# One transformer layer in split fp32: the first feed-forward chunk as seven block products, and modulation sums of 1024 columns

## The chip, the cores and the metric

The kernel runs on one NeuronCore of one Trainium2 chip. The metric is the device time of one execution in microseconds; of several executions the median counts. TensorE (PE) does matrix products, with its weight loads beside them (PEld); VectorE (DVE), ScalarE (ACT) and GpSimd (POOL) do elementwise work; SyncE (SP) and POOL issue most DMAs. Each engine runs its own instructions in order and waits for others at semaphores, so the order of the rows on each engine is part of the kernel.

## The reference, cut to what matters

One layer of a diffusion backbone is computed for 640 tokens: 128 context tokens and 512 latent ones, which share the weights but have modulations of their own (`c_ctx` and `c`). D_MODEL is 1024, D_FF 4096.

```python
def _modulation(cvec, w_mod, b_mod):
    m = jax.nn.silu(cvec) @ w_mod + b_mod
    return jnp.split(m[:, None, :], N_MOD, axis=-1)
...
    sh1, sc1, g1, sh2, sc2, g2 = _modulation(c, w_mod, b_mod)
    h = _rmsnorm(x, n1) * (1 + sc1) + sh1
...
    x = x + g1 * _merge(a_o, b_o, ga, gb, w_br_a, w_br_b, w_out)
    h2 = _rmsnorm(x, n2) * (1 + sc2) + sh2
    return x + g2 * _mlp(h2, w1, w2)
```

`_mlp` is a squared ReLU between two products: `relu(h2 @ w1)**2 @ w2`. A last RMSNorm follows. Everything is fp32.

## The kernel before, in words

**Data.** Activations lie feature-major: a tile holds 128 features of all 640 tokens, so a 1024-wide activation is eight tiles, f = 0 to 7. Tokens fall into two halves of 320, h0 and h1; h0 holds the 128 context tokens and 192 latent ones, and since their modulations differ, a modulated operation on h0 is a pair of 128 and 192 columns (`SEGS`). PE gets its precision by a split: each operand is a rounded high part and a low part (the rest), and a product of a 128x128 weight with 128x320 is three matmuls: high x high, high x low, low x high. ACT makes a weight's high part (L267, L1395), DVE or POOL its low part by a subtraction (L276, L273, L1400).

**Stages.** The input projection and two attentions fill the time to about 400 us. A merge follows: for each feature n two branch units per half, gated and added on DVE, whose sum is split into mh (ACT) and ml (DVE). From 449 us the output projection runs in units: `unit` (L1199) is 24 matmuls, eight k with three each, into one PSUM bank, called pss, pt or pg in rotation. Its order is features 0 to 3 with both halves, then h0 of 4 to 7, then h1 of 4 to 7. Behind each unit DVE adds the gated result to the residual x (`add_gated`, L1224), ACT squares it (L201), DVE sums the squares (L203). When a half is complete, two matmuls with ones (L208, L209), a logarithm and an exponential on ACT (L210, L211) make rstd, and the norm and modulation follow in steps on DVE and ACT: x times rstd and scale (xm, L336), high part with the shift added (hh0h to hh7h, L341), low part (hh0l to hh7l, L344).

**Late modulation.** The second half of the modulation map isn't done by PE. For each of 32 column tiles DVE multiplies rows of w_mod with a broadcast silu(cond) and sums along the row (L1102), in two halves of 512 columns for each of two conditions; `mods_done` adds the halves. `mod_pace` hands these sums out between the units by a running account of DVE time, MCOST a step; what is left is done when a step needs it.

**Feed-forward.** D_FF is worked off in four chunks of 1024. Layer 1 of chunk 0 was 16 plain units (eight output tiles, two halves), their weights through the class `Weights` (W), their ReLU and square into `hid_raw(0, ...)` (blocks 11, 12, 21, 22 by output parity and half). Everything after that runs as block products of Strassen's kind in Winograd's form, in the order of the list `SEQ`: a layer of a chunk is seen as 2x2 blocks (weight blocks by parity and k half, activation blocks by k half and token half) and done in seven products A11, A12, S3, A22, S2, S1, S4 instead of eight, each for n = 0 to 3. A product is 12 matmuls (four k with three each) into a bank of the eight-bank pool pp8. Its weights come through the class `Operands` (`OPS[0]`): A tiles are plain, B tiles are sums of two weight blocks, loaded by SP and added to by a DMA that POOL issues. Its activations are blocks and sums of blocks (B11, B21, T1 to T4, N22). For layer 1 these operands come from the split normed features: `t_pieces` adds hh-high and hh-low again, forms the differences and splits them anew, in small steps in the list `side`, of which one is taken after each product. POOL makes the low parts of A12 and A22 in layer 1.

**Order.** Up to `manual.close()` DVE's order is the order of the code; in the kernel before that call comes within or behind the plain feed-forward units. The other engines' order, and DVE's afterwards, is set by a list scheduler at build time.

Of the kernel before, what the change touches and what calls it, by code (L numbers as in the profile page):

```python
# [10 lines left out]
F32 = mybir.dt.float32  # L11
# [17 lines left out]
WP1 = 0  # L29
# [9 lines left out]
MCOST = 1500  # L39
LAG = (0, 4)  # L40
# [33 lines left out]
def trunk_layer(ctx: ExitStack, tc: tile.TileContext, xT, small_in, wmodA, wmodB, tabs, cacheK, cacheV, bias,  # L74
# [43 lines left out]

    def tt_tile(name):
        return cur["p"].tile([P, NT], F32R, tag="tt", bufs=12, name=name)  # L120
# [85 lines left out]
    def rstd_half(acc, last, rstd, sl):  # L206
        p, n = ps_t(), sl.stop - sl.start
# [3 lines left out]
        ACT.activation(rstd[:, sl], rstd[:, sl], AF.Exp, scale=-0.5)  # L211


    def w_order():
# [10 lines left out]
        for n in range(KT):  # L225
            yield ("w1", n), w1[n]
# [79 lines left out]
    WPOOLSET = {("out", n) for n in range(WPO, KT)} | {("w1", n) for n in range(WP1)}  # L306
    EXTRA = {("out", 4), ("w1", 0)}
# [781 lines left out]
    def late_mods():  # L1089

        cb = [tt_tile("cb") for _ in range(4)]
        for i in range(2):
            for q in range(2):
                MISC.dma_start(r32(cb[2 * q + i][:, :512]),
                               silu[i, 4 * q:4 * q + 4].rearrange("k p -> (k p)").partition_broadcast(P))
        for n in MODS:
            st = dp.tile([P, 1024], F32, tag="ms", bufs=3, name="wmt")
            DQ[QM].dma_start(st, wmodB[n])
            for q in range(2):
                for i in range(2):  # L1100
                    t = dp.tile([P, 512], F32, tag="mt", bufs=2, name="mt")
                    DVE.scalar_tensor_tensor(t, st[:, q * 512:(q + 1) * 512], 1.0, r32(cb[2 * q + i][:, :512]), op0=OP.mult,  # L1102
                                             op1=OP.mult, accum_out=parts[:, q, n, i:i + 1])
                if q == 0:
                    yield
# [121 lines left out]
    def norm_pieces(acc, last, rstd, h, apply):  # L1227
        return [lambda: None] * LAG[h] + [lambda: rstd_half(acc, last, rstd, HALVES[h])] + [lambda f=f: apply(range(f, min(f + NG, KT)))
                                                     for f in range(0, KT, NG)]

    def norm2(fs, h):
        mod_step(16 + 4 * (fs.stop + -fs.stop % MG) - lm_n[0])
        modulate([(H2[f], X1[f], mod(2, f), mod(1, f)) for f in fs], rstd2, h)

    X1 = {}
    acc2, rstd2 = u("acc2"), u("rstd2")
    H2 = [h_pair(f"hh{f}") for f in range(KT)]
    Wt = {}
    for n, h in order(KT, 4):
        if n not in Wt:  # L1240
            Wt[n] = W.get("out", n)
            X1[n] = o_tile(f"x1_{n}")
            nc.sync.dma_start(X1[n], xT[:, n, :])
        ps = unit(Wt[n], M, h)
        if h:
            W.done("out", n)
        add_gated(n, ps, h, 0)
        sq = sq_add(acc2, X1[n], n, HALVES[h])
        if n < KT - 4 or h == 0 and n < KT - 1:
            mod_pace(OU)  # L1250
        elif n == KT - 1:
            side += norm_pieces(acc2, sq, rstd2, h, lambda fs, h=h: norm2(fs, h))

    def final(fs, sl):
        for f in fs:
            DVE.tensor_mul(X1[f][:, sl], X1[f][:, sl], rstd3[:, sl])
            (nc.sync, nc.scalar)[f % 2].dma_start(yT[:, f, sl], X1[f][:, sl])

    def relu2(dst, src, h):

        r, sl = u("rl"), HALVES[h]
        ACT.activation(r[:, :HT], src, AF.Relu)
        if RL:
            ACT.activation(r[:, :HT], r[:, :HT], AF.Square)
            ACT.activation(dst[0][:, sl], r[:, :HT], AF.Copy)
        else:
            ACT.activation(dst[0][:, sl], r[:, :HT], AF.Square)

        def rest():
            if not RL:
                DVE.tensor_mul(r[:, :HT], r[:, :HT], r[:, :HT])
            DVE.tensor_sub(dst[1][:, sl], r[:, :HT], r32(dst[0][:, sl]))
        flush_later(posts)
        posts.append(rest)


    T = [{}, {}, {}]
    L0, L1 = slice(0, HT), slice(HT, NT)  # L1280

    def t_pieces(k):
        raw = {}

        def cut(dst, src, sl0, sl1):
            ACT.activation(dst[0][:, sl0], src, AF.Copy)
            later.append(lambda: DVE.tensor_sub(dst[1][:, sl1], src, r32(dst[0][:, sl0])))

        def p0():
            if k == 2:  # L1290
                mod_step(64 - lm_n[0])
            for i in range(3):
                T[i][k] = tt_tile(f"t{i + 1}_{k}")
            for i in range(2):
                raw[i] = u("hr")
                DVE.tensor_add(raw[i], r32(H2[k + 4 * i][0]), r32(H2[k + 4 * i][1]))
            raw[2] = u("t12")
            DVE.tensor_sub(raw[2][:, L0], raw[0][:, L1], raw[0][:, L0])
            cut((T[0][k], T[0][k]), raw[2][:, L0], L0, L1)
# [491 lines left out]
```

## Time and profile before

| | |
|---|---|
| runs shown | 928.15, 922.33, 924.48 us; median 924.48 |
| profiled execution | 927.14 us, of which the span of instructions 925.4 us |
| granted PE clock, mean | 0.996 |
| busy | PE 98%, PEld 95%, DVE 77%, ACT 61%, POOL 21% |
| DMA | 150.04 MB, mean 162 GB/s |

A row of the timeline gives the start in microseconds from the start of the span, the duration, the engine, the line of the kernel, the operation, result and operands by the program's names, and the shapes; a bracket at the end is the idle time ahead of it and what ended it. Matmuls overlap in the pipe, and so do, a little, instructions of DVE and ACT: the cost of one in a row of them is the distance of the starts. PEclk is the clock that PE was granted. A row of the windows gives, for a stretch of time, each engine's busy time and number of instructions.

### The profile page before, as it was taken

Reading aid. Unit: us, or ns where it says so; the run is one execution under the profiler, and the core shown is the slowest. Engines: PE = TensorE matmul, PEld = TensorE weight load, DVE = VectorE, ACT = ScalarE, POOL = GpSimd, SP = SyncE. Lnnn points to the kernel's source line nnn. Section 1 sums busy time; section 2 is a strip of 40 time slices with the busy share of each in tenths; the row PEclk is TensorE's granted clock in tenths of the full one; section 3 lists DMA queues with packets and bytes.
Section 4 is the critical chain, followed back from the end, with each engine's and each line's share of the span. In section 5 each row is a group of like instructions: output and inputs, shape, how many; then the busy total and the mean of one; then the engine's idle time right before and its main releaser. Section 6 shows DMA issues by size and latency. Waiting matters only on the chain.

```text
span 925.4 us, 16638 instructions
## 1 busy us (share of the span) xinstructions
PE 907.2 (98%) x6136; PEld 874.9 (95%) x6136; DVE 713.1 (77%) x1505; ACT 563.7 (61%) x1174; POOL 194.7 (21%) x224
## 2 busy tenths in 40 slices
PE   9999999999999999999999999999999999999996
PEld 7799889989999999999999999999999999999995
DVE  6675877857766697586789996985798769975897
ACT  4566767757656775665324667536764576447775
POOL 0020200002211011111130010354134532354140
PEclk9999999999999999999999999999999999999999
DMA  9883410115636389788843463898678876897575
GB/s 345 304 238 103 93 42 26 57 56 154 166 103 154 115 261 286 185 236 250 273 138 91 124 172 102 130 205 182 158 141 188 182 164 157 175 175 177 100 123 151
DMA packets 54177, 150.04 MB, mean 162 GB/s; under 512 B 6672, under 2 KB 10400, under 8 KB 54096
## 3 DMA queue, kind: packets, MB, share of 16 engines
q1 hardware_dynamic: 31440, 99.74, 32.5%
q0 software_dynamic: 21504, 47.93, 29.7%
q10 hardware_dynamic: 1152, 1.31, 0.4%
q8 instruction: 48, 0.79, 0.4%
q14 instruction: 33, 0.27, 0.1%
HBM read 136.62 MB, written 4.60 MB: 153 GB/s over the span
## 4 chain that ended last, share of the span: by engine, by line
PE 74%; DMA 8%; DVE 7%; ACT 5%; issue 4%; POOL 1%; SPq 0%; DVEq 0%; POOLq 0%; ACTq 0%
PE b L1659 10%; PE b L1660 10%; PE b L1658 10%; PE pg L315 6%; PE pg L316 6%; PE pg L317 6%; DMA wsb<-w 3%; PE pss L317 3%; PE pss L316 3%; PE pss L315 3%; PE pt L317 2%; PE pt L316 2%; PE pt L315 2%; DVE mt L1102 2%; PE pt L694 1%
## 5 line engine op out<-in xcount | busy, mean ns | idle before, releaser
L1395 ACT ACTIVATE wb<-wsb 128x512 fp32r<-128x512 f32 x140 | 87.0, 628 | 93.8 <-PE b L1660 57.7
L1659 PE MATMUL b<-op,wb 128*128 128x320 f32 x448 | 138.7, 310 | 1.3 <-DVE op L1468 1.3
L1658 PE MATMUL b<-op,wb 128*128 128x320 f32 x448 | 138.6, 309 | 0.6 <-ACT op L1467 0.6
L1660 PE MATMUL b<-op,wb 128*128 128x320 f32 x448 | 138.4, 309 | 0.0
L1400 DVE TENSOR_TENSOR wb<-wsb,wb 128x512 fp32r<-128x512 f32 x124 | 91.4, 740 | 32.3 <-ACT wb L1395 32.1
L1403 POOL DMA_DIRECT2D wsb<-w x84 | 73.7, 908 | 128.0 <-DVE wb L1400 99.8
L1659 PEld LDWEIGHTS b<-op,wb 128*128 128x128 f32 x448 | 84.1, 188 | 2.1 <-DVE op L1468 2.1
L1102 DVE SCALAR_TENSOR_TENSOR mt<-wmt,cb 128x512 f32<-128x512 f32 x128 | 80.7, 687 | 6.3 <-DMA wmt<-wmodB 6.2
L1658 PEld LDWEIGHTS b<-op,wb 128*128 128x128 f32 x448 | 84.2, 188 | 1.2 <-ACT op L1467 0.9
L1660 PEld LDWEIGHTS b<-op,wb 128*128 128x128 f32 x448 | 84.1, 188 | 0.0
L267 ACT ACTIVATE wh<-wst 128x512 fp32r<-128x512 f32 (+1 forms) x84 | 61.0, 740 | 32.9 <-PE pg L316 12.9
L276 DVE TENSOR_TENSOR wl<-wst,wh 128x512 fp32r<-128x512 f32 (+1 forms) x57 | 44.4, 789 | 15.0 <-ACT wh L267 13.0
L1380 POOL DMA_DIRECT2D wsb<-w x28 | 26.4, 944 | 139.0 <-DMA wsb<-w 51.7
L633 DVE TENSOR_TENSOR pl<-pt,ph 128x512 fp32r<-128x512 f32 (+1 forms) x72 | 44.9, 627 | 13.6 <-ACT ph L632 13.1
L632 ACT ACTIVATE ph<-pt 128x512 fp32r<-128x512 f32 (+1 forms) x72 | 39.2, 548 | 15.5 <-PE po L702 5.4
L1511 DVE SCALAR_TENSOR_TENSOR x<-b,parts,x 128x128 f32<-128x128 f32 (+1 forms) x116 | 46.3, 429 | 2.5 <-PE b L1660 1.6
L1658 PE MATMUL b<-t,wb 128*128 128x320 f32 x144 | 44.8, 311 | 0.4 <-DVE tp L1497 0.4
L1659 PE MATMUL b<-t,wb 128*128 128x320 f32 x144 | 44.5, 309 | 0.0
L1660 PE MATMUL b<-t,wb 128*128 128x320 f32 x144 | 44.5, 309 | 0.0
L1395 ACT ACTIVATE wb<-wst 128x512 fp32r<-128x512 f32 x56 | 34.7, 625 | 15.8 <-PE b L1660 8.8
L1468 DVE TENSOR_TENSOR op<-hid,op 128x1280 fp32r<-128x1280 f32 (+2 forms) x32 | 37.0, 1155 | 7.8 <-ACT op L1467 7.7
L1511 DVE SCALAR_TENSOR_TENSOR x<-tp,parts,x 128x320 f32<-128x320 f32 (+2 forms) x60 | 39.0, 679 | 1.0 <-ACT tp L1562 1.0
(886 smaller groups left out, 3010.2 us busy)
## 6 DMA issues: line engine op xcount, KB each, us to landing
wsb<-w POOLq DMA_DIRECT2D x112, 256.0 KB, 5.2
wst<-w SPq DMA_DIRECT2D x36, 512.0 KB, 3.9
wmt<-wmodB SPq DMA_DIRECT2D x32, 512.0 KB, 5.0
wst<-w_in SPq DMA_DIRECT2D x31, 512.0 KB, 4.2
wsb<-w SPq DMA_DIRECT2D x28, 512.0 KB, 4.3
ms<-wmodA SPq DMA_DIRECT2D x16, 512.0 KB, 7.7
wl<-w_in POOLq DMA_DIRECT2D x8, 512.0 KB, 7.8
wst<-w_br SPq DMA_DIRECT2D x8, 512.0 KB, 5.0
```

Source lines behind the costliest of these rows:

```text
L267: ACT.activation(hi[:, ks], st[:, ks], AF.Copy)
L315: PE.matmul(ps, wh[:, k], xh[:, sl], start=first, stop=False)
L316: PE.matmul(ps, wh[:, k], xl[:, sl], start=False, stop=False)
L317: PE.matmul(ps, wl[:, k], xh[:, sl], start=False, stop=last)
L1102: DVE.scalar_tensor_tensor(t, st[:, q * 512:(q + 1) * 512], 1.0, r32(cb[2 * q + i][:, :512]), op0=OP.mult, op1=OP.mult, accum_out=parts[:, ...
L1395: ACT.activation(w[:, 0:4], t, AF.Copy)
L1400: (nc.gpsimd if o in BLKPOOL[l - 1] else DVE).tensor_sub(w[:, 4:8], t, r32(w[:, 0:4]))
L1403: nc.gpsimd.dma_start(t, self.src(l, c, n, e)[:, 4 * half:4 * half + 4], accum_op=OP.add)
L1511: DVE.scalar_tensor_tensor(X1[i][:, sl], src[:, sl.start - off:sl.stop - off], g[:, j:j + 1], X1[i][:, sl], op0=OP.mult, op1=OP.add)
L1658: PE.matmul(b, w[:, k], xh, start=not whole and k == 0, stop=False, skip_group_check=True)
L1659: PE.matmul(b, w[:, k], xl, start=False, stop=False, skip_group_check=True)
L1660: PE.matmul(b, w[:, 4 + k], xh, start=False, stop=o not in ("A11", "S2", "S1") and k == 3, skip_group_check=True)
```

## The change

1. Layer 1 of chunk 0 goes through the seven block products too. The weights w1 of chunk 0 leave `Weights`; `FIRST0` begins with 28 products, among them three A11 products of layer 2 between S3 and S2. The four S3 products form a group: k 0 and 1 of all four, then k 2 and 3 of all four. In layer 2 of chunk 0, A12 gets a bank of its own and is added to the kept A11 by DVE (four more additions).
2. The operands come from unrounded normed features. `norm_first` (h0, four steps of two features) and `norm_last` (h1, four steps of two) scale on DVE and shift on ACT into raw tiles; `cut` splits a raw tile into parts on ACT and DVE; `t3_piece`, `t2_piece`, `t4_piece`, `t1_piece`, `n22_piece` form the differences from the raw tiles.
3. The modulation sums take 1024 columns each, 64 instead of 128 of 512; MCOST goes from 1500 to 1300 a step; all that are left are done with unit (6,0) of the output projection, where before the last of them ran beside the feed-forward units.
4. The PSUM pool of the units is closed, and pp8 opened, right behind the output projection; `manual.close()` moves there too. The pool of B tiles opens at unit (5,1).

```diff
         for n in range(KT):
             yield ("out", n), w_out[n]
-        for n in range(KT):
-            yield ("w1", n), w1[n]
...
     def mods_done(n0, n1):
         m = mods[:, n0:n1]
-        DVE.tensor_add(m, parts[:, 0, n0:n1], parts[:, 1, n0:n1])
...
-            for q in range(2):
-                for i in range(2):
-                    t = dp.tile([P, 512], F32, tag="mt", bufs=2, name="mt")
-                    DVE.scalar_tensor_tensor(t, st[:, q * 512:(q + 1) * 512], 1.0, r32(cb[2 * q + i][:, :512]), op0=OP.mult,
-                                             op1=OP.mult, accum_out=parts[:, q, n, i:i + 1])
-                if q == 0:
+            for i in range(2):
+                t = dp.tile([P, 1024], F32, tag="mt", bufs=1, name="mt")
+                DVE.scalar_tensor_tensor(t, st, 1.0, cb[i], op0=OP.mult, op1=OP.mult, accum_out=mods[:, n, i:i + 1])
+                if i == 0:
                     yield
...
+    def scaled(t, f, h):
+
+        off = HALVES[h].start
+        for sl, g in SEGS[h]:
+            d = t[:, sl.start - off:sl.stop - off]
+            DVE.scalar_tensor_tensor(d, X1[f][:, sl], mod(2, f)[:, g:g + 1], rstd2[:, sl], op0=OP.mult, op1=OP.mult)
+
+    def shifted(t, f, h):
+        off = HALVES[h].start
+        for sl, g in SEGS[h]:
+            d = t[:, sl.start - off:sl.stop - off]
+            ACT.activation(d, d, AF.Identity, bias=mod(1, f)[:, g:g + 1])
+
+    def norm_first(f0):
+
+        mod_step(16 + 4 * (f0 + 2) - lm_n[0])
...
+        for f, t in todo:
+            shifted(t, f, 0)
+            cut(H2[f][0][:, L0], H2[f][1][:, L0], t)
...
+    def cut(hi, lo, src):
+        ACT.activation(hi, src, AF.Copy)
+        later.append(lambda: DVE.tensor_sub(lo, src, r32(hi)))
...
+    def t3_piece(k):
+        r = t_new(2, k)
+        DVE.tensor_sub(r, RAW1[0][:, k + 4], RAW1[0][:, k])
+        cut_t(2, k, r)
...
-    FIRST0 = [("A11", 0), ("A11", 1), ("A11", 2), ("A12", 0), ("A12", 1), ("A11", 3), ("A12", 2), ("A12", 3)]
+    FIRST0 = [("A11", 0, 1), ("A11", 1, 1), ("A11", 2, 1), ("A12", 0, 1), ("A12", 1, 1), ("A11", 3, 1), ("A12", 2, 1),
+              ("A12", 3, 1), ("S3", 0, 1), ("S3", 1, 1), ("S3", 2, 1), ("S3", 3, 1), ("A11", 0), ("A11", 1), ("A11", 2),
+              ("S2", 0, 1), ("S2", 1, 1), ("S2", 2, 1), ("A22", 0, 1), ("S2", 3, 1), ("A22", 1, 1), ("A22", 2, 1),
+              ("A22", 3, 1), ("S1", 0, 1), ("S1", 1, 1), ("S4", 0, 1), ("S1", 2, 1), ("S4", 1, 1), ("S1", 3, 1),
+              ("S4", 2, 1), ("S4", 3, 1), ("A12", 0), ("A11", 3), ("A12", 1), ("A12", 2), ("A12", 3)]
...
             mod_pace(OU)
-        elif n == KT - 1:
-            side += norm_pieces(acc2, sq, rstd2, h, lambda fs, h=h: norm2(fs, h))
+        elif n == KT - 1 and h == 0:
+            side += [rstd2_half(sq, 0)] + [lambda f=f: norm_first(f) for f in range(0, KT, 2)]
+        if (n, h) == (5, 1):
             mod_step(64 - lm_n[0])
             pairs_pool()
...
     manual.close()
     banks.close()
     pp8.append(ctx.enter_context(tc.tile_pool(name="pp8", bufs=1, space=bass.MemoryType.PSUM, reuse_waits="tile")))
...
+    side += [lambda: None] * LAG2 + [rstd2_half(sq, 1)]
+    side += steps((norm_last, 0)) + steps((norm_last, 1), (t3_piece, 0)) + steps((norm_last, 2), (t3_piece, 1))
+    side += steps((norm_last, 3), (t3_piece, 2)) + steps((t3_piece, 3))
+    for f in (t2_piece, t4_piece, t1_piece, n22_piece):
+        for k in range(4):
+            side += steps((f, k))
```

Three places show how the rows move.

**PE, where the output projection ends.** pt is the bank of its last unit, (7,1); before, the next rows are plain feed-forward units, which read hh tiles and a weight w. With the waits of each row, before:

```order
L317 MATMUL pt<-mh,wl 128x320
L315 MATMUL pss<-hh0h,w_6148 128x320 [waits PE_49,Activation_49]
L316 MATMUL pss<-hh0l,w_6148 128x320 [waits DVE_49]
L317 MATMUL pss<-hh0h,w_6149 128x320 [waits DVE_49]
L315 MATMUL pss<-hh1h,w_6148 128x320 [waits Activation_49]
L316 MATMUL pss<-hh1l,w_6148 128x320
L317 MATMUL pss<-hh1h,w_6149 128x320
L315 MATMUL pss<-hh2h,w_6148 128x320 [waits Activation_49]
L316 MATMUL pss<-hh2l,w_6148 128x320 [waits DVE_49]
```

In the changed kernel b is a bank of pp8 and wb a block product's weight:

```order
L323 MATMUL pt<-mh,wl 128x320
L1646 MATMUL b<-hh0h,wb 128x320 [waits DVE_49,Activation_49]
L1647 MATMUL b<-hh0l,wb 128x320
L1648 MATMUL b<-hh0h,wb 128x320
L1646 MATMUL b<-hh1h,wb 128x320
L1647 MATMUL b<-hh1l,wb 128x320
L1648 MATMUL b<-hh1h,wb 128x320
L1646 MATMUL b<-hh2h,wb 128x320 [waits Activation_49]
L1647 MATMUL b<-hh2l,wb 128x320
L1648 MATMUL b<-hh2h,wb 128x320
L1646 MATMUL b<-hh3h,wb 128x320 [waits Activation_49]
L1647 MATMUL b<-hh3l,wb 128x320
```

Before, the first matmul waits for PE and ACT, and each low part's reader for DVE by itself. Now the first matmul waits for DVE, and the readers of hh0l to hh3l carry no wait for DVE any more.

**DVE, up to the gated add of unit (6,1).** x_6 is the residual of feature 6, xm a scaled feature, wl a plain weight's low part; before:

```order
L344 SCALAR_TENSOR_TENSOR hh5l<-xm,parts,hh5h 128x128
L344 SCALAR_TENSOR_TENSOR hh5l<-xm,parts,hh5h 128x192
L276 TENSOR_TENSOR wl<-wst,wh 128x1024
L1224 SCALAR_TENSOR_TENSOR x_5_6001<-pg,parts,x_5_6001 128x320
L1102 SCALAR_TENSOR_TENSOR mt,parts<-wmt,cb 128x512
L203 TENSOR_TENSOR acc_5642<-acc_5642,sq 128x320
...
L344 SCALAR_TENSOR_TENSOR hh7l<-xm,parts,hh7h 128x128
L344 SCALAR_TENSOR_TENSOR hh7l<-xm,parts,hh7h 128x192
L276 TENSOR_TENSOR wl<-wst,wh 128x1024
L1224 SCALAR_TENSOR_TENSOR x_6_6033<-pss,parts,x_6_6033 128x320
```

In the changed kernel, where raw is an unrounded feature and wb a block product's low part:

```order
L1391 TENSOR_TENSOR wb<-wst,wb 128x512 x2
L1225 SCALAR_TENSOR_TENSOR x_5_5902<-pg,parts,x_5_5902 128x320
L211 TENSOR_TENSOR acc_5560<-acc_5560,sq 128x320
L1601 TENSOR_SCALAR parts<-parts 128x16
L1274 TENSOR_TENSOR hh2l<-raw,hh2h 128x320
L1274 TENSOR_TENSOR hh3l<-raw,hh3h 128x320
L1274 TENSOR_TENSOR hh4l<-raw,hh4h 128x320
L1274 TENSOR_TENSOR hh5l<-raw,hh5h 128x320
...
L1240 SCALAR_TENSOR_TENSOR raw<-x_7_5973,parts,rstd_5561 128x192
L1391 TENSOR_TENSOR wb<-wst,wb 128x512
L1225 SCALAR_TENSOR_TENSOR x_6_5938<-pss,parts,x_6_5938 128x320
```

The gated add of (6,1) stands behind the low parts of hh2 to hh5, the scaling of features 6 and 7 and three low parts of block products; the modulation sums between are gone.

**DVE, ahead of the output projection.** sg and ml are the merge of feature 7; wl is a low part of an output weight. Before:

```order
L276 TENSOR_TENSOR wl<-wst,wh 128x1024
L1102 SCALAR_TENSOR_TENSOR mt,parts<-wmt,cb 128x512 x6
L1181 TENSOR_TENSOR sg<-pg,sg 128x320
L1181 TENSOR_TENSOR sg<-pss,sg 128x320
L1182 TENSOR_TENSOR sg<-sg 128x320
L1184 TENSOR_TENSOR ml<-sg,mh 128x320
```

In the changed kernel:

```order
L282 TENSOR_TENSOR wl<-wst,wh 128x1024
L1104 SCALAR_TENSOR_TENSOR mt,parts<-wmt,cb 128x1024 x4
L1182 TENSOR_TENSOR sg<-pg,sg 128x320
L1182 TENSOR_TENSOR sg<-pss,sg 128x320
L1183 TENSOR_TENSOR sg<-sg 128x320
L1185 TENSOR_TENSOR ml<-sg,mh 128x320
```

Six sums of 512 columns ahead of the merge of feature 7 became four of 1024.

More of the change, by code (lines that the diff above doesn't have):

```diff
@@ L38 @@
 NG = 2
[L39 to L40 removed]
+MCOST = 1300
+LAG2 = 2
 MAN = (0,)
@@ L1256, in final @@
[L1256 to L1276, printed above, removed]
@@ L1686, in trunk_layer @@
             side.pop(0)()
+    OPS[0].ahead()
+    todo = list(SEQ)
+    while todo:
+        group = [todo.pop(0)]
+        while todo and group[0][:2] == todo[0][:2] == (1, 0) and group[0][3] == todo[0][3] == "S3":
+            group.append(todo.pop(0))
+        jobs = []
+        for x in group:
+            l, c, n, o = x
+            w = OPS[0].get(x)
+            if l == 1:
+                xk = XN[o]
+            else:
+                t = opd(c, XOF[o])
+                xk = lambda k, t=t: (t[:, k], t[:, 4 + k])
+            p = pairs.setdefault((l, c, n), Pair())
+            whole = {"A12": "A11", "S1": "S2", "S4": "S2"}.get(o)
+            if (l, c, o) == (2, 0, "A12"):
+                whole = None
+            b = getattr(p, "b" + whole) if whole else bank()
+            setattr(p, "b" + o, b)
+            jobs.append((b, w, xk, o, whole, (l, c, n, o, b, p)))
+        if len(jobs) > 1:
+            flush_later()
+            for b, w, xk, o, whole, _ in jobs:
+                product(b, w, xk, o, whole, range(2))
+        for b, w, xk, o, whole, e in jobs:
+            product(b, w, xk, o, whole, range(2 if len(jobs) > 1 else 0, 4))
+            evict(*e)
     while side:
```

199 lines of the change are left out of this document (87 added, 112 removed).

## The prediction

> **What bounds the kernel now.** I read the page first: its span, the busy time by engine, the forty slices.
>
> ```profile
> span 925.4 us, 16638 instructions
> PE   907.2 (98%) x6136; PEld 874.9 (95%) x6136; DVE 713.1 (77%) x1505; ACT 563.7 (61%) x1174; POOL 194.7 (21%) x224
> PE   9999999999999999999999999999999999999996
> DVE  6675877857766697586789996985798769975897
> PEclk9999999999999999999999999999999999999999
> ```
>
> PE is busy in every slice at a full granted clock; no other engine is near that in the mean, though DVE comes close in slices 22 to 24, 486 to 555 us. Next I took the windows around the change: the output projection, the first feed-forward chunk, the products behind it (columns: stretch, length, busy time and instructions of PE, PEld, DVE, ACT, POOL, then clock, DMA share and GB/s).
>
> ```profile
> 449.00:507.00 58.00, 58.00 (x394) 57.68 (x393) 47.87 (x123) 20.80 (x39) 9.64 (x4) 1.00 0.50 165
> 507.00:563.00 56.00, 55.88 (x376) 54.98 (x375) 49.31 (x100) 34.36 (x73) 3.46 (x4) 1.00 0.45 123
> 563.00:617.00 54.00, 54.00 (x370) 54.00 (x369) 49.28 (x90) 31.15 (x56) 18.95 (x21) 1.00 0.77 162
> ```
>
> PE idles 0.12 us in these 168. So there is no stall for the change to recover: a gain can come only from matmuls that are no longer issued, and every wait that it adds shows in full. DVE is at 88% in the stretch that is rewritten, so its order decides whether PE stays fed.
>
> **What is removed.** Sixteen units of 24 matmuls become 28 products of 12: 384 - 336 = 48 fewer, and the rows of PE's order bear that out (5323 matmuls of 128x320 before, 5275 after). The group row offers a price, the timeline another:
>
> ```profile
> L1659 PE MATMUL b<-op,wb 128*128 128x320 f32 x448 | 138.7, 310 | 1.3 <-DVE op L1468 1.3
> 480.92 0.31 PE L315 MATMUL pss<-mh,wh 128*128 128x320 f32 x1
> 484.44 0.31 PE L315 MATMUL pg<-mh,wh 128*128 128x320 f32 x1
> 506.64 0.31 PE L315 MATMUL pss<-hh0h,w 128*128 128x320 f32 x1
> ```
>
> The mean of 310 ns is the time in which one matmul is in the pipe; two overlap. From 480.92 to 484.44 PE starts a whole unit of 24, so one costs 3.52/24 = 0.1467 us. The removed work is worth 48 x 0.1467 = **7.0 us**, not 48 x 0.31 = 14.9. That is 0.8% of 924, and about 1% is what a measurement of this kernel can tell from no change. The third row is the hand-over: the first feed-forward matmul starts at 506.64, right behind the last unit of the output projection.
>
> **What DVE's work does to the hand-over.** In the kernel before DVE is far behind there, and PE doesn't care:
>
> ```profile
> 513.09 0.54 DVE L1224 SCALAR_TENSOR_TENSOR x<-pss,parts,x 128x320 f32<-128x320 f32 x1
> 515.78 0.55 DVE L1224 SCALAR_TENSOR_TENSOR x<-pt,parts,x 128x320 f32<-128x320 f32 x1
> ```
>
> These are the gated adds of units (6,1) and (7,1), the last two of the output projection: 6.5 and 9.1 us after PE had passed on. The feed-forward units took banks of the same PSUM pool that were free, and the first four read only the first token half. In the changed kernel the pool is closed behind the output projection and the eight-bank pool opened, so the first product, A11(0), gets a bank that (6,1) still fills, and the third, A11(2), that of (7,1). The order shows it: A11(0)'s first matmul carries a wait on DVE, and the rows behind it, which read hh1l to hh3l, carry none, since the wait already reaches past these rows on DVE, to the gated add that is listed behind hh5l. So the time of that gated add is the first term, and I price DVE's and ACT's rows up to it by start-to-start times.
>
> ```profile
> 495.08 0.47 ACT L211 ACTIVATE rstd<-rstd 128x320 f32<-128x320 f32 x1
> 502.16 1.27 DVE L336 SCALAR_TENSOR_TENSOR xm<-x,parts,rstd 128x128 f32<-128x128 f32 x4
> 503.34 0.68 DVE L344 SCALAR_TENSOR_TENSOR hh2l<-xm,parts,hh2h 128x128 fp32r<-128x128 f32 x2
> 522.07 0.55 DVE L344 SCALAR_TENSOR_TENSOR hh2l<-xm,parts,hh2h 128x320 fp32r<-128x320 f32 x1
> 522.54 0.55 DVE L336 SCALAR_TENSOR_TENSOR xm<-x,parts,rstd 128x320 f32<-128x320 f32 x1
> 448.17 0.48 DVE L1181 TENSOR_TENSOR sg<-pg,sg 128x320 f32<-128x320 f32 x1
> 448.57 0.48 DVE L1181 TENSOR_TENSOR sg<-pss,sg 128x320 f32<-128x320 f32 x1
> 597.11 0.69 DVE L1400 TENSOR_TENSOR wb<-wsb,wb 128x512 fp32r<-128x512 f32 x1
> 597.71 0.67 DVE L1511 SCALAR_TENSOR_TENSOR x<-b,parts,x 128x128 f32<-128x128 f32 x2
> ```
>
> A pair of 128 and 192 columns costs 1.18/2 = 0.59, a scalar-tensor-tensor of 320 0.46, a tensor-tensor of 320 0.40, a weight's low part 0.60. The first half's rstd is there at 495.55, as before. DVE then has eight scale pairs (4.7), the gated adds (4,1) and (5,1) (0.9), two accumulations, six low parts hh0l to hh5l (3.2 together) and three weight low parts (1.8): 10.6 us, so 506.2 if it never waited. But it waits for ACT three times.
>
> ```profile
> 497.15 0.73 ACT L341 ACTIVATE hh0h<-xm,parts 128x128 fp32r<-128x128 f32 x2
> 497.79 0.73 ACT L341 ACTIVATE hh1h<-xm,parts 128x128 fp32r<-128x128 f32 x2
> 516.87 0.45 ACT L201 ACTIVATE sq<-x 128x320 f32<-128x320 f32 x1
> 517.23 0.42 ACT L1483 ACTIVATE hid<-pg 128x320 f32<-128x320 f32 x1
> 620.80 0.62 ACT L1395 ACTIVATE wb<-wst 128x512 fp32r<-128x512 f32 x1
> 621.32 0.62 ACT L1395 ACTIVATE wb<-wsb 128x512 fp32r<-128x512 f32 x1
> ```
>
> ACT's shift of a pair costs 0.64, a copy or square 0.36, a weight conversion 0.52. In its order the conversion of A11(1) stands behind the shifts and copies of features 2 to 5. ACT starts on feature 2 at about 500.4, when DVE has scaled it; four shift pairs, three copies and a conversion (4.2) later it reaches the second conversion, done at 505.2; DVE stood before its low part from 502.6. With 1.2 before the square of (4,1) and 0.7 before that of (5,1) the waits come to 4.5, and the gated add of (6,1) starts at about 510.8 and ends at 511.4. PE, free at 506.64, idles **4.8 us**.
>
> POOL makes it more. It has the low parts of A12(0) and A12(1), from about 506.7, when DVE is in hh2l to hh5l. Nearest row:
>
> ```profile
> 622.71 2.83 DVE L1400 TENSOR_TENSOR wb<-wsb,wb 128x512 fp32r<-128x512 f32 x2
> 622.78 1.60 POOL L1400 TENSOR_TENSOR wb<-wst,wb 128x512 fp32r<-128x512 f32 x1
> ```
>
> Two such instructions of DVE take 0.60 + 0.69 = 1.29 alone; beside one of POOL 2.83, a loss of 1.54. Bounds for two: 0 (POOL comes at another moment) to 3.1. I take one loss, 1.5, since DVE's remaining waits swallow part. First term: 6.3 us, ends 4.8 and 7.9 (0 if the waits for ACT don't arise). [...]
>
> **A second price of the idle time** is PE's clock. Once in this trace PE got half of it:
>
> ```profile
> 130.28 0.50 PE L702 MATMUL po<-ph,vst 128*128 128x512 f32 x1 [0.72 <-ACT ph L632]
> 131.88 0.38 PE L315 MATMUL pg<-h0h,wh 128*128 128x320 f32 x1 [0.87 <-DVE qs L577]
> 132.69 0.45 PE L317 MATMUL pg<-h1h,wl 128*128 128x320 f32 x1
> 136.12 0.31 PE L315 MATMUL pg<-h6h,wh 128*128 128x320 f32 x1
> ```
>
> After idle times of 0.72 and 0.87 us, thirteen matmuls from 132.69 to 136.12 took 3.43 us where 13 x 0.1467 is 1.91: 1.5 lost. Behind a stall of six I expect the same once: **1.5** (0 to 1.7). [...]
>
> **The start of the output projection.** Its first unit reads ml of feature 7 in its last three matmuls:
>
> ```profile
> 450.75 1.51 DVE L1184 TENSOR_TENSOR ml<-sg,mh 128x320 fp32r<-128x320 f32 x1 [1.17 <-ACT mh L1183]
> 452.47 0.31 PE L316 MATMUL pss<-ml,wh 128*128 128x320 f32 x1
> 489.84 0.69 DVE L1102 SCALAR_TENSOR_TENSOR mt<-wmt,cb 128x512 f32<-128x512 f32 x1
> 490.45 0.69 DVE L1102 SCALAR_TENSOR_TENSOR mt<-wmt,cb 128x512 f32<-128x512 f32 x1
> ```
>
> ml lands at 452.26, 0.2 us ahead. A modulation sum of 512 columns costs 0.61. No row has 1024; between one and two of 512 (0.61 to 1.22) I take 1.15, nearest to two. Over the last weight low part ahead of the merge there are four sums of 1024 (4.6) where six of 512 stood (3.7): 0.9 later, less the slack, plus what the copy on ACT and POOL's instruction next to it add. I take **1.0**, 0 to 1.5. All the sums together save DVE 64 x 0.07 = 4.5 us, on an engine that isn't the bound.
>
> **The rest of layer one.** From the gated add of (7,1) on, DVE has 58 instructions until the last low part that A22(0) reads: 11 scalar-tensor-tensors, 11 weight low parts, 35 tensor-tensors of 320 and one of 960 (about 1.1 by their size), 5.1 + 6.6 + 14.0 + 1.1 = 26.8 us without a pause. Laid beside PE's products in their order, PE waits 0.2 for the second low part of T3, 0.6 for the third, 0.4 for the operand of the layer-two filler and 0.4 for T4: **1.6** (0 to 3). What the unrounded operands save, adding high and low part again, lay off PE's path and counts nothing.
>
> **Sum:** 1.0 + 6.3 + 1.5 + 1.6 = 10.4 added, 7.0 removed: +3.4. The profiled execution took 927.14 us, 2.7 above the median of the runs shown, 924.48; on the median I predict 924.5 + 3.4 = **927.9**. Its own range, by the ends of the terms, is 922 to 932.
>
> **Rivals.** (a) *The hand-over holds.* For it: DVE's work alone ends at 506.2, just ahead of PE; ACT is at 61% on the page, and if its shifts run ahead of DVE's list the gated add is in time. Then no first stall and no half clock: 1.0 + 1.6 - 7.0 = -4.4, 920.1; if the small waits vanish too, 917.5. Against it: the conversion of A11(1) stands behind work that DVE itself feeds. Chance 0.24. (b) *POOL's blocking goes on.* DVE has no pause between 518 and 546, so each further low part on POOL (A12(2), A12(3), then A22) costs PE its 1.54 one for one. The first stall at its upper end (+1.6) and three such blocks (+4.6) give 927.9 + 6.2 = 934.1, slower by over 1%. It decides once POOL's share ahead of A22(0) exceeds the pauses that DVE still has. Against it: POOL wasn't beside DVE in most rows of its kind. Chance 0.17. (c) *The price per removed matmul is wrong.* If the 48 gave 14.9 us the time would be about 920; the starts speak clearly against it. 0.02. The change's not taking effect is excluded by the order.
>
> **Chances.** 0.57 for my sum. Faster by over 1% (under 915.3) needs more than the whole removed work: 0.03. Slower by over 1% (over 933.7): most of (b) and the edge of my sum, 0.12. Within: 0.85. The range 918.5 to 934 takes in most of (a) and the foot of (b).
>
> **What would show it.** In the trace after: an idle time of 5 to 8 us on PE at about 507, ended by the gated add from pss; thirteen slow matmuls behind it; the third product close behind the add from pt; about a microsecond at 452; small waits of S3 and A22 for DVE; from 563 on the same pace as before. If PE goes on at 507 without a pause, (a) holds; if DVE's low parts near 507 and 519 take 2 us and more, (b).

## The result and the profile after

The changed kernel took 936.79 us (median of four executions, 934.38 to 938.76) against 925.22 of the kernel before, a ratio of 1.0124 with a 95% interval of 1.0083 to 1.0164: slower by 1.2%, where 927.9 was forecast in a range up to 934.0. Its profiled execution is the quickest of its four, 934.38 us with a span of 932.6, so the traces account for 7.2 us of the loss; the 2 to 4 us by which the other executions were longer are in no trace.

The page of the changed kernel, its span, the busy times and the slices:

```profile
span 932.6 us, 16531 instructions
PE   904.7 (97%) x6088; PEld 871.9 (93%) x6088; DVE 718.0 (77%) x1383; ACT 572.8 (61%) x1202; POOL 218.9 (23%) x246
PE   9999999999999999999997989999999999999996
DVE  6675777857666788597786798976798868986897
```

PE has 48 instructions fewer, and now two of its slices ahead of the last are below nine, the 22nd and the 24th (490 to 513 and 536 to 560 us). The windows of the same kernel, columns as before:

```profile
449.00:507.00 58.00, 57.67 (x389) 56.86 (x388) 41.40 (x79) 21.82 (x46) 13.86 (x8) 1.00 0.59 179
507.00:563.00 56.00, 47.44 (x294) 46.07 (x294) 48.97 (x94) 39.17 (x88) 21.11 (x20) 0.91 0.55 105
563.00:617.00 54.00, 52.75 (x360) 52.47 (x359) 49.02 (x88) 32.13 (x55) 16.06 (x19) 1.00 0.79 174
617.00:700.00 83.00, 81.15 (x542) 80.69 (x541) 61.84 (x100) 50.67 (x94) 33.80 (x35) 0.98 0.80 167
```

In the second row PE starts 294 matmuls where 376 ran before, its clock is 0.91, and POOL is busy for 21.1 us instead of 3.5. The rows of PE's timeline that end a wait:

```profile
452.88 0.41 PE L321 MATMUL pss<-mh,wh 128*128 128x320 f32 x1 [0.22 <-ACT mh L1184]
513.90 0.61 PE L1646 MATMUL b<-hh0h,wb 128*128 128x320 f32 x1 [6.05 <-DVE x L1225]
548.48 0.90 PE L1646 MATMUL b<-t,wb 128*128 128x320 f32 x2 [2.24 <-ACT t L1273]
595.85 0.41 PE L1648 MATMUL b<-op,wb 128*128 128x320 f32 x1 [1.25 <-DVE wb L1391]
639.54 0.42 PE L1646 MATMUL b<-t,wb 128*128 128x320 f32 x1 [1.85 <-DVE tp L1493]
```

I counted, in both traces, the time between starts of matmuls of 128x320 beyond 0.1467 us each. Up to 449 us the two are level to 0.2: the output projection's first matmul starts at 449.25 before and at 449.43 after. From 449 to 563 it is 1.6 before and 14.4 after; from 563 to 617, 0.0 and 1.5; from 617 to 700, 1.6 and 3.8; behind 700, 4.3 and 1.8. That is 14.3 us more in all, less the 7.0 of the removed matmuls: 7.3, against the 7.2 of the spans. Of the 12.9 between 449 and 563, 0.9 lie at the start of the output projection, 6.2 in the stall at 507, 1.6 in the twelve slow matmuls behind it (granted clock 0.50 from 513.9 to 517.3), 2.8 in the waits at 544 and 548, 1.5 in the slow matmuls behind those.

What DVE and POOL did in the first stall and ahead of the second, in their timelines:

```profile
507.13 2.75 POOL L1391 TENSOR_TENSOR wb<-wst,wb 128x512 fp32r<-128x512 f32 x2 [5.55 <-ACT wb L1386]
507.38 1.38 DVE L211 TENSOR_TENSOR acc<-acc,sq 128x320 f32<-128x320 f32 x1 [0.61 <-ACT sq L209]
508.68 1.23 DVE L1601 TENSOR_SCALAR parts<-parts 128x16 f32<-128x16 f32 x1
513.22 0.54 DVE L1225 SCALAR_TENSOR_TENSOR x<-pss,parts,x 128x320 f32<-128x320 f32 x1
...
542.15 1.63 POOL L1391 TENSOR_TENSOR wb<-wsb,wb 128x512 fp32r<-128x512 f32 x1
542.43 1.92 DVE L1391 TENSOR_TENSOR wb<-wsb,wb 128x512 fp32r<-128x512 f32 x1
545.07 2.44 DVE L1507 SCALAR_TENSOR_TENSOR x<-tp,parts,x 128x320 f32<-128x320 f32 x1
545.23 1.93 POOL L1391 TENSOR_TENSOR wb<-wsb,wb 128x512 fp32r<-128x512 f32 x1
547.44 0.48 DVE L1289 TENSOR_TENSOR tp<-op 128x320 f32<-128x320 f32 x1
547.95 0.47 ACT L1273 ACTIVATE t<-tp 128x320 fp32r<-128x320 f32 x1 [3.39 <-DVE tp L1289]
```

The gated add of (6,1) starts at 513.22, right ahead of PE's restart. Each of these DVE instructions beside one of POOL ends no earlier than that one: the weight's low part takes 1.92 us instead of 0.69, the gated add 2.44 instead of 0.54. The blocked gated add holds up DVE's subtraction of tp at 547.44; ACT's t at 547.95 waits for that, and PE for t until 548.48. No wait of PE between 449 and 700 us was ended by POOL itself, so by the profile it isn't the lateness of POOL's own low parts that PE meets.

### The profile page after: what moved, and what is told of

It reads as the page before. It is cut to its first block, busy times and chain, and to the rows that moved or that the text cites. A ratio compares the mean times of both kernels' runs of the same rounds, so it can differ in the third digit from the quotient of the medians.

```text
span 932.6 us, 16531 instructions
## 1 busy us (share of the span) xinstructions
PE 904.7 (97%) x6088; PEld 871.9 (93%) x6088; DVE 718.0 (77%) x1383; ACT 572.8 (61%) x1202; POOL 218.9 (23%) x246
## 4 chain that ended last, share of the span: by engine, by line
PE 76%; DVE 10%; ACT 5%; issue 3%; DMA 3%; POOL 1%; DVEq 0%; SPq 0%; ACTq 0%; POOLq 0%
PE b L1646 10%; PE b L1647 10%; PE b L1648 10%; PE pg L321 6%; PE pg L322 6%; PE pg L323 6%; PE pss L322 2%; PE pss L321 2%; PE pss L323 2%; DVE wb L1391 2%; PE pt L322 2%; PE pt L321 2%; PE pt L323 2%; PE pt L700 1%; PE pss L413 1%
## 5 line engine op out<-in xcount | busy, mean ns | idle before, releaser
L1386 ACT ACTIVATE wb<-wsb 128x512 fp32r<-128x512 f32 x160 | 99.2, 628 | 99.6 <-PE b L1648 59.7
L1391 DVE TENSOR_TENSOR wb<-wsb,wb 128x512 fp32r<-128x512 f32 x140 | 103.4, 742 | 35.8 <-ACT wb L1386 35.3
L1394 POOL DMA_DIRECT2D wsb<-w x96 | 84.8, 919 | 129.2 <-DVE wb L1391 94.7
L1104 DVE SCALAR_TENSOR_TENSOR mt<-wmt,cb 128x1024 f32<-128x1024 f32 x64 | 78.2, 1222 | 6.3 <-DMA wmt<-wmodB 5.1
L273 ACT ACTIVATE wh<-wst 128x512 fp32r<-128x512 f32 (+1 forms) x77 | 53.6, 711 | 28.6 <-PE pg L322 12.3
L1646 PE MATMUL b<-t,wb 128*128 128x320 f32 x192 | 59.9, 318 | 4.1 <-ACT t L1273 2.2
L1647 PE MATMUL b<-t,wb 128*128 128x320 f32 x192 | 60.8, 317 | 0.3 <-DVE t L1274 0.2
L1648 PE MATMUL b<-t,wb 128*128 128x320 f32 x192 | 60.4, 315 | 0.0
L1371 POOL DMA_DIRECT2D wsb<-w x32 | 29.6, 926 | 107.4 <-DMA wsb<-w 31.2
L1386 ACT ACTIVATE wb<-wst 128x512 fp32r<-128x512 f32 x64 | 39.9, 625 | 16.1 <-PE b L1648 8.9
L282 DVE TENSOR_TENSOR wl<-wst,wh 128x512 fp32r<-128x512 f32 (+1 forms) x50 | 35.8, 728 | 12.2 <-ACT wh L273 9.9
L1646 PEld LDWEIGHTS b<-t,wb 128*128 128x128 f32 x192 | 36.8, 194 | 5.0 <-ACT t L1273 2.5
```

The costliest lines, as they stand in the source:

```text
L273: ACT.activation(hi[:, ks], st[:, ks], AF.Copy)
L1104: DVE.scalar_tensor_tensor(t, st, 1.0, cb[i], op0=OP.mult, op1=OP.mult, accum_out=mods[:, n, i:i + 1])
L1386: ACT.activation(w[:, 0:4], t, AF.Copy)
L1391: (nc.gpsimd if o in BLKPOOL[l - 1] else DVE).tensor_sub(w[:, 4:8], t, r32(w[:, 0:4]))
L1394: nc.gpsimd.dma_start(t, self.src(l, c, n, e)[:, 4 * half:4 * half + 4], accum_op=OP.add)
L1646: PE.matmul(b, w[:, k], xh, start=not whole and k == 0, stop=False, skip_group_check=True)
```

## The experiments

Theory A: DVE's order holds up the last gated adds. Theory B: POOL's subtractions block DVE. Theory C: the half clock follows from PE's idleness. Theory D: DVE has too much work for PE's shorter stretch. Ratios are to the kernel before on the same chip. A span is that of one execution: the wait of PE at about 452 us, ahead of which the changed kernel and the runs built on it do the same, ended between 451.4 and 453.6 us. So 2 us between two spans say little, and the ratios decide.

**One norm step per unit** (A against B).

```diff
-            side += [rstd2_half(sq, 0)] + [lambda f=f: norm_first(f) for f in range(0, KT, 2)]
+            side += [rstd2_half(sq, 0)] + [q for f in range(0, KT, 2) for q in (lambda f=f: norm_first(f), lambda: None)][:-1]
```

> The first-half norm steps of the output projection are issued one per unit instead of two, so that the gated adds of (5,1), (6,1), (7,1) stand earlier in DVE's order; the same instructions otherwise. Theory A (DVE's order holds up the last gated adds, and with them the PSUM banks): the stall of 6.2 us at 507 falls under 1.5 us, no half clock follows, span 932.6 - 4.7 - 1.5 = about 926. Rival B (POOL's low parts block DVE whatever the order): at least 3 us of the stall stay, span 929 or more.

932.03 us, 1.0054 (1.0032 to 1.0076), span 927.5. The stall shrank from 6.05 to 2.33 us, between the two expectations (under 1.5; 3 or more): DVE's order sets most of it, and POOL's subtraction at 504.78 still stretched hh3l to 1.58 us (0.48 in the changed kernel, at 510.23, where no subtraction of POOL ran). The row of PE:

```profile
509.00 0.60 PE L1646 MATMUL b<-hh0h,wb 128*128 128x320 f32 x1 [2.33 <-DVE x L1225]
```

**Low parts of A12 and A22, chunk 0, on DVE** (B against D).

```diff
-                (nc.gpsimd if o in BLKPOOL[l - 1] else DVE).tensor_sub(w[:, 4:8], t, r32(w[:, 0:4]))
+                (nc.gpsimd if o in BLKPOOL[l - 1] and ((l, c) != (1, 0) or o not in ("A12", "A22")) else DVE).tensor_sub(w[:, 4:8], t, r32(w[:, 0:4]))
```

> The low parts of A12 and A22 in layer 1 of chunk 0 are made by DVE, not by POOL (eight subtractions of 128x512). Theory B (POOL's subtractions block DVE's instructions for their whole length): at 507 DVE loses 2 us less and works 1.2 us more, so the first stall goes from 6.2 to about 5.4; at 542 to 548 DVE loses 3.3 us less and works 1.2 more, so the stall of 2.2 us there and the half clock behind it go; span 932.6 - 0.8 - 2.4 - 1.3 = about 928. Rival (DVE is simply full there): eight more instructions of 0.6 us on DVE, the stalls grow, span 934 to 937.

933.84 us, 1.0069 (1.0043 to 1.0094), span 931.8. The local forecast of B held: the first stall fell to 4.70 (5.4 expected), the wait at 548 is gone. The span gained less than 1 us where 4.6 were expected: PE's excess between 563 and 617 rose from 1.5 to 4.2 and behind 800 from 1.7 to 3.4. Here the work moved, it did not vanish. The two DVE rows that were blocked are short again:

```profile
507.78 0.49 DVE L211 TENSOR_TENSOR acc<-acc,sq 128x320 f32<-128x320 f32 x1 [0.61 <-ACT sq L209]
508.19 0.17 DVE L1601 TENSOR_SCALAR parts<-parts 128x16 f32<-128x16 f32 x1
```

**PE kept busy in the stall** (C).

```diff
+    wu = un.ps()
+    for _ in range(36):
+        PE.matmul(wu, Wt[7][0][:, 0], M[0][0][:, :HT], start=True, stop=True)
     v_pool.close()
```

> Thirty-six idle matmuls of 128x320 (5.3 us, result unused) are put on PE behind the output projection, where it waits. Theory C (the half clock behind the stall is due to PE's idleness): the first products run at 0.147 us a matmul instead of 0.267, 1.5 us less there, nothing else changes, span about 931.1. Rival (the clock falls for another reason, or the idle matmuls delay the first product): 932.6 or more.

935.66 us, 1.0085 (1.0055 to 1.0114), span 930.2; the median can't be told from the changed kernel's. The first products ran at 0.147 us a matmul, 0.267 in the changed kernel:

```profile
512.78 0.31 PE L1650 MATMUL b<-hh0h,wb 128*128 128x320 f32 x1
512.92 0.30 PE L1651 MATMUL b<-hh0l,wb 128*128 128x320 f32 x1
...
546.78 0.57 PE L1650 MATMUL b<-t,wb 128*128 128x320 f32 x2 [2.22 <-ACT t L1273]
547.19 0.31 PE L1651 MATMUL b<-t,wb 128*128 128x320 f32 x1
```

So idleness is the cause there. Unexpected: the stall of 2.22 us at 546.78 is as long as the one at 548.48 of the changed kernel (2.24), and no half clock follows it: the clock granted from 507 to 563 was 1.00, against 0.91 in the changed kernel.

**Three banks passed over.**

```diff
     pp8.append(ctx.enter_context(tc.tile_pool(name="pp8", bufs=1, space=bass.MemoryType.PSUM, reuse_waits="tile")))
+    for _ in range(3):
+        bank()
```

> Three banks of the new PSUM pool are passed over, so that the first products get banks that no late unit fills. If the bank is the only gate of the first product: the stall goes, span about 925. Theory A (DVE's order is the cause, the bank only the place where it shows): the first product then waits for its own low parts, hh2l and hh3l (done at 510.7 in the trace after), a stall of about 3 us, and the rstd matmul for the square of feature 7 (517.7), another 2 to 3 us; the sum of both within 1 us of 6.2; with the shorter pauses the half clock may stay away: span 930.5 to 933.

935.76 us, 1.0098 (1.0061 to 1.0134), span 931.9. The first product waited 6.05 us for the same gated add, as without the edit: the three tiles that nothing writes did not move it, and the edit tells nothing of banks. It stands as a second measurement of the changed kernel.

**Gated adds first, one norm step per unit** (A in full).

```diff
-        if side:
+        if side and tail:
             side.pop(0)()
...
-        ps = unit(Wt[n], M, h)
+        ps = unit(Wt[n], M, h, False)
+        add_gated(n, ps, h, 0)
+        if side:
+            side.pop(0)()
+        sq = sq_add(acc2, X1[n], n, HALVES[h])
         if h:
             W.done("out", n)
-        add_gated(n, ps, h, 0)
-        sq = sq_add(acc2, X1[n], n, HALVES[h])
```

> As the run with one norm step per unit, and in addition each gated add stands ahead of the unit's norm step and of the next weights' low parts in DVE's order. Same instructions. Theory A: both last gated adds start within a microsecond of their units' ends, so the stall at 507, 6.2 us in the changed kernel and 2.3 us with one step per unit, falls under 1 us, and no half clock follows there. Against the run with one step per unit: 2.3 + 1.5 - 0.8 = 3 us less, span about 924.5. If POOL's low parts alone hold DVE up there, 1.5 us or more of the stall stay.

933.39 us, 1.0092 (1.0061 to 1.0123), span 931.1. The stall at 507 is gone, as A said, and nearly nothing came of it: the span, forecast at 924.5, is 1.5 us under the changed kernel's and 3.6 over that with one norm step per unit alone. The first two waits of PE in that stretch, and its window:

```profile
512.17 0.38 PE L1648 MATMUL b<-hh0h,wb 128*128 128x320 f32 x1 [0.27 <-DVE x L1225]
524.43 0.41 PE L1648 MATMUL b<-hh4h,wb 128*128 128x320 f32 x1 [2.14 <-ACT hid L1483]
...
507.00:563.00 56.00, 50.24 (x327) 47.90 (x326) 52.38 (x99) 43.47 (x99) 22.89 (x23) 1.00 0.64 123
```

A wait of 2.1 us turned up at 524, 2.2 at 544, and others followed: between 510 and 563 PE lost 8.3 us. DVE is at 52.4 of 56 us from 507 to 563. So it seems that the first stall was only the first place at which PE met that backlog.

**The same, without POOL's subtractions**: ACT writes the negated high part, a DMA adds the weight.

```diff
-            if (l, c) == (2, 3) and (o, n) in LOTAIL:
+            if (l, c) == (2, 3) and (o, n) in LOTAIL or (l, c) == (1, 0) and o in ("A12", "A22"):
```

> As the run before, and the eight low parts of A12 and A22 in layer 1 of chunk 0 are made without POOL's subtraction: ACT writes the negated high part and a DMA adds the weight to it. DVE's work stays the same, ACT has eight conversions more. Theory B (POOL's subtractions blocked DVE, which has no pause there): the stall of 2.2 us at 544 to 548 goes, with what stands behind it, and DVE is ahead by 3 us from then on, so that the waits at 595 and 639 (1.4 and 2.0 us) shrink too: span 3 to 6 us under the run before, about 920. Rival (DVE's amount of work sets it, and what is gained at 548 comes back as waits up to 640, as in the run with DVE's own low parts): within 1.5 us of the run before.

934.71 us, 1.0098 (1.0061 to 1.0135), span 935.6. The blocking made way for the DMA: its landing ended two waits.

```profile
552.96 0.43 PE L1650 MATMUL b<-hh0h,wb 128*128 128x320 f32 x1 [1.76 <-DMA wb<-wsb]
559.64 0.42 PE L1650 MATMUL b<-hh0h,wb 128*128 128x320 f32 x1 [1.37 <-DMA wb<-wsb]
```

**The same edit on the changed kernel alone.**

> The changed kernel with only this edit: the eight low parts of A12 and A22 in layer 1 of chunk 0 through ACT and a DMA, not by POOL. Theory B: the first stall falls from 6.2 to about 4.2 (DVE loses 2 us less at 507), the one at 548 goes; span 932.6 - 2 - 2.8 = about 928, and less if the half clock behind them stays away. Theory A with DVE's amount as the second limit: only the first stall's 2 us, span about 930.5.

941.23 us, 1.0185 (1.0132 to 1.0238): the slowest of all. The first stall fell to 4.10 and the one at 548 went, as B said, and DMA waits of 0.5 to 2.1 us took their place. Neither run decides B.

**The kernel before with the 1024-wide sums alone.**

> The kernel before with one part of the change alone: the late modulation sums of 1024 columns (64 instead of 128 of 512) and no adding of parts; everything else, MCOST too, as before. If the sums cost what was estimated (1.15 us against 1.22), DVE has 4 us less work and PE, which is fed either way, does not notice but for up to 1 us at the start of the output projection: within 1.5 us of the kernel before. If this part is what costs time: slower by 2 us or more.

928.08 us, 1.0034 (1.0011 to 1.0058), span 924.4, 1 us under that of the kernel before. By the ratio, of ten executions, this part costs about 3 us. The profiled execution, the third quickest of them, shows the same loss in place: PE's excess from 449 to 563 is 4.6 us against 1.6, with waits for hh4l, hh6h and a weight's low part. It is won back behind 617, where none of the sums lies.

```profile
507.00:563.00 56.00, 54.47 (x356) 52.02 (x355) 47.98 (x94) 34.42 (x72) 3.48 (x4) 1.00 0.42 123
617.00:700.00 83.00, 83.00 (x568) 83.00 (x567) 67.59 (x112) 53.92 (x98) 33.24 (x34) 1.00 0.80 166
```

Nor did the sums become cheaper. Two that follow each other start 1.26 us apart, here and in the changed kernel, whose rows are these; two of 512 take 2 x 0.61 = 1.22. The 64 sums cost DVE about 2.6 us more at that distance than the 128 did, where 4.5 less were forecast. Why there is a gap between accumulator read and next sum, 0.04 us in the rows below, which those of 512 don't have (in the kernel before, a read and the next sum both start at 490.45), wasn't tested; the product tile mt has one buffer now instead of two.

```profile
444.68 1.22 DVE L1104 SCALAR_TENSOR_TENSOR mt<-wmt,cb 128x1024 f32<-128x1024 f32 x1
445.82 0.08 DVE L1104 DVE_READ_ACCUMULATOR mt<-wmt,cb 128x1 f32 x1
445.94 1.23 DVE L1104 SCALAR_TENSOR_TENSOR mt<-wmt,cb 128x1024 f32<-128x1024 f32 x1
```

**Low parts left out** on the kernel with gated adds first. In each of three runs the third matmul reads the high part again, so PE's work stays the same: POOL's eight left out, DVE's twenty, and both. The edit of the first; the other two name the other five products, and all seven.

```diff
-            else:
+            elif (l, c) != (1, 0) or o not in ("A12", "A22"):
                 (nc.gpsimd if o in BLKPOOL[l - 1] else DVE).tensor_sub(w[:, 4:8], t, r32(w[:, 0:4]))
```

> On the kernel with gated adds first and one norm step per unit (span 931.1): the eight low parts that POOL makes (A12 and A22 in layer 1 of chunk 0) are left out; their third matmul reads the high part again, so PE's work is the same. Theory B (POOL blocks DVE): POOL's four subtractions at 506 to 518 and four at 538 to 549 cost DVE 5 to 7 us there; without them the waits at 524, 544 and 549 (2.3, 2.4 and 0.9 us) go for the most part, span about 926. Theory D (DVE has too much work of its own for PE's 50 us of products there, POOL aside): under 2 us, span 929 or more.

923.35 us, 0.9979 (0.9957 to 1.0001), span 924.4. The waits at 544 and 549 are gone; the first one, at 524, stays at 1.8 us, ended by ACT's eviction.

> On the same kernel: the twenty low parts that DVE makes for layer 1 of chunk 0 (A11, S3, S2, S1, S4; 12 us of DVE's work) are left out, POOL's eight stay. Theory D (DVE's amount of work): the waits between 524 and 640 (10 us together) go, span about 922 to 923. Theory B alone: POOL's blocking stays, the wait at 544 stays over 1.5 us, span 927 or more.

928.76 us, 1.0038 (1.0012 to 1.0065), span 927.7. Each expectation held in one half: the wait at 544 is gone, as D said, though waits of 1.5 us at 523 and 2.0 at 634 stay; the span is over 927, as B said.

> On the same kernel: all twenty-eight low parts of layer 1 of chunk 0 are left out. If elementwise work (DVE's amount and POOL's blocking together) is all that took the gain of the 48 matmuls, PE runs through from 454 to the end as in the kernel before and the span is the kernel before's less 7.0 plus 0.8 at the start of the output projection: about 919 to 920. If 923 or more, something else (ACT, DMA, banks) takes a part.

923.71 us, 0.9974 (0.9951 to 0.9997), span 923.2. Against 1.0092 with all low parts, POOL's eight are worth 1.1%, DVE's twenty 0.5%, both 1.2%. Windows of the run without POOL's and of that without both:

```profile
507.00:563.00 56.00, 54.21 (x356) 53.48 (x355) 47.33 (x100) 46.62 (x104) 12.99 (x15) 0.97 0.65 145
...
507.00:563.00 56.00, 55.13 (x371) 54.27 (x371) 38.72 (x85) 47.27 (x108) 13.04 (x16) 1.00 0.68 153
```

With DVE's twenty in place and POOL's gone, DVE is at 47.3 of 56 us and PE is busy for 54.2. So the amount on DVE alone isn't the limit; POOL's blocking on top of it is, and the wait at 544 goes when either is taken away. With both gone the span is still 3 to 4 us above the 919 to 920 expected, so that something else takes a part.

**POOL's low parts moved to DVE, with gated adds first**: chunk 0 alone, then all chunks (`BLKPOOL = ((), ())`), then all chunks in the kernel before.

> The kernel with gated adds first and one norm step per unit, complete again, with the low parts of A12 and A22 of layer 1 of chunk 0 on DVE instead of POOL (eight subtractions of 0.60 us). Theory B (POOL's blocking took the gain): as in the run without POOL's low parts (924.4), with up to 2 us for DVE's 4.8 us of added work: span 924 to 927. Theory D (DVE's amount): back at the span with POOL's (931) or more, as when the same move was made alone (931.8).

928.33 us, 1.0020 (0.9994 to 1.0046), span 923.4. This keeps all work: 0.72% under the kernel with POOL's subtractions, with intervals that don't meet, although DVE has 4.8 us more to do. It decides for B, where the gated adds come first. Of the 7.7 us between the two spans 2.0 lie ahead of PE's wait at 452 us, where the two do the same.

> The same with no low part on POOL in any chunk (32 subtractions go to DVE). What stayed open is the 3 us between 563 and 700 that the run without any low part in chunk 0 still lost, with waits at 586 and 630. If POOL's blocking in layer 1 of chunk 1 makes the wait at 630 (DVE's gated adds take 3.7 us there beside POOL), that wait of 2 us goes: span 2 us under the run with chunk 0 alone. If DVE's amount decides: the same or more.

924.87 us, 1.0008 (0.9985 to 1.0032), span 926.5. The median is lower, the span higher; by the intervals the two are not told apart. The wait at 630 stayed, so POOL's blocking was not its cause. In this run it goes back to ACT, which waits for a weight pair; its row:

```profile
630.53 1.15 ACT L1386 ACTIVATE wb<-wsb 128x512 fp32r<-128x512 f32 x2 [2.67 <-DMA wsb<-w]
```

> The kernel before with the low parts that POOL makes (24 in layer 1 of chunks 1 to 3) on DVE. If POOL's blocking costs PE nothing where DVE has cover, within 1.5 us of the kernel before; if it costs there too, up to 1.6 us faster (the kernel before lost 1.6 us between 617 and 700 and 1.1 between 700 and 800); if DVE's amount decides, slower.

924.04 us, 0.9998 (0.9977 to 1.0019). Its window:

```profile
617.00:700.00 83.00, 83.00 (x568) 83.00 (x567) 67.58 (x119) 53.40 (x96) 22.09 (x26) 1.00 0.78 164
```

PE has no wait left between 617 and 700, but that can't be put down to the edit: the kernel before with the 1024-wide sums, whose POOL makes its low parts, has none there either (83.00 of 83.00 above). No time followed that can be measured: where PE's work covers DVE's, the blocking costs little. No complete version beat the kernel before; that with all low parts on DVE equals it.

## Why the prediction was wrong, and where it was right

- **What bounds the kernel, and the price of a matmul**: right. 48 x 0.1467 = 7.0 closes the sum of the traces to 0.1 us; the mean duration of 310 ns would have left 8 us unexplained.
- **The hand-over**: right in mechanism and size. Forecast 6.3 us, ended by the gated add from pss; measured 6.2. That the size is so near is in part luck: DVE waited 3.6 us for ACT where 4.5 were forecast, lost 2.0 to POOL instead of 1.5, and the sum of its own work, 10.6, leaves out the two accumulations that it lists (0.8). One norm step per unit and gated adds first took it away without changing a matmul.
- **The half clock behind it**: right there (1.5 forecast, 1.6 measured), wrong in number. It came three times, behind 513.9, 548.5 and 639.5, 4.6 us in all. No run shows the 1.7 at the upper end of its range: each of the three cost 1.5 or 1.6.
- **The start of the output projection**: 1.0 forecast, 0.9 measured. The four sums alone took 4.95 us where 4.6 were forecast.
- **"The rest of layer one", 1.6 (0 to 3): this step failed.** The prediction held that DVE has no pause between the gated add of (7,1) and A22, and still priced its 58 rows at their undisturbed 26.8 us, with POOL's blocking entered once, ahead of them. DVE did have a pause, 4.8 us ahead of 522.04; POOL's low parts of A12(2) and A12(3), at 518.64 and 520.33, fell into it, and the small waits of S3 forecast for about 530 didn't come. POOL's low parts of A22, at 542.15 and 545.23, met a DVE without pause: they made the wait of 2.2 us at 548.48 and, with the wait at 544 and the half clock behind, the cost was 4.3. That is 2.7 more than forecast.
- **Rival (b)** had the mechanism for A22, and deserved more than 0.17. Its price was right only by chance: it wanted the first stall at 7.9 and three blocks, and the traces show 6.2 and a cost for A22 alone. Its 934.1, on the median, is near the 934.38 of the profiled execution, but the median is 936.79.
- **What no trace shows.** The median missed the forecast by 8.9 us. The traces show 3.8 of them, most in the rest of layer one (2.7) and behind 563 us (1.2). Of the others, 2.7 are that by which the profiled execution before lay above the median of the runs shown, and 2.4 that by which the changed kernel's lay under its own.
- **"From 563 on the same pace as before": also wrong.** PE lost 1.5 us more from 563 to 617 and 2.2 more from 617 to 700, and lost 2.5 less later. That last difference may be one of executions: the kernel before with the 1024-wide sums lost as little there (1.5 behind 700, against 4.3 and 1.8). Waits at 583 to 600 and 628 to 644 stayed in every run with the change. One was traced to a late weight pair in one run; their cause as a whole stays open.
- **The difference in kind**: I added up waits along the changed kernel's rows, as if one removed would be won. The run without the first stall shows that they aren't additive: PE runs up against the same elementwise backlog a few products later. That 16 plain units covered it in the kernel before, where 28 products of half the length don't, is read from the windows (PE fed, DVE at 49.3 of 56 us); no run tests it by itself.
- **The 1024-wide sums**: 1.15 forecast, 1.26 measured, more than two of 512. They were taken for harmless; alone they made the kernel before 0.3% slower. How much of the changed kernel's loss is theirs stays open: no run has the rest of the change with sums of 512.

## What to carry to other kernels

When PE is the bound and loses work, the first question is what elementwise work that PE time covered, and whether it still fits; count an engine's rows with the blocking of its neighbour in them wherever it has no pause (here a gated add of 0.54 us took 2.44 beside POOL). Test a stall by taking it away before adding it to a sum: if the backlog is the cause, microseconds come back at the next operands: with the first stall of 6.05 us gone, PE still lost 8.3 between 510 and 563. An engine that helps another may cost it more than the work that it takes over: with the gated adds first, eight subtractions on POOL cost the kernel 0.7% more than the same eight on DVE. In the changed kernel itself the same move gained 0.3 to 0.6%, not clear of the noise.

## What the runs showed of the hardware

- A short DVE instruction with one small operand was blocked as well: L1601, 128x16, took 1.23 us beside POOL and 0.17 in the run without POOL's subtraction there.
- The half clock came behind short pauses too. After an idle time of 1.85 us (639.54) it began 0.9 us after PE had restarted; after 2.22 us (546.78, the run with PE kept busy) it didn't come. The rows of the changed kernel around its third slow stretch:

```profile
640.24 0.39 PE L1647 MATMUL b<-t,wb 128*128 128x320 f32 x1
640.42 0.47 PE L1648 MATMUL b<-t,wb 128*128 128x320 f32 x1
643.62 0.36 PE L1648 MATMUL b<-t,wb 128*128 128x320 f32 x1
643.82 0.31 PE L1646 MATMUL b<-t,wb 128*128 128x320 f32 x1
```

The slow stretch, 640.42 to 643.82, lasted 3.40 us, at a granted clock of 0.52 from 640.4 to 643.9. The idle times of PE ahead of the three were 6.05, 2.24 and 1.85 us. What decides which pause brings the half clock, no run here shows.
